# Half-block products of a hybrid attention layer: block sums taken out from beside them, one of four sums added by VectorE

## The chip, the cores and the metric

The kernel runs on one core of a Trainium2 chip. The metric is the device time of one execution in microseconds. Five engines work side by side, each in its own order: TensorE (PE, the matmuls, and PEld, its weight loads), VectorE (DVE), ScalarE (ACT), GpSimd (POOL) and SyncE (SP). SP issues nearly all DMAs, POOL those that accumulate in flight or write operands away to DRAM. Each engine waits in front of an instruction until its operands and buffers are there, and everything behind it waits too.

## What is computed

One decoder layer on 512 tokens of width 2048, in float32: RMS norm, one input projection, eight heads of latent attention (MLA) and eight of forgetting attention (FoX), each gated with SiLU, one output projection, RMS norm, residual.

```python
h = rms_norm(x, g_pre)
q_lat, kv_lat, k_rope, gate_mla, fq, fk, fv, f_logit, gate_fox = split(h @ w_in)
q  = rms_norm(q_lat, g_q) @ w_uq
kv = rms_norm(kv_lat, g_kv) @ w_ukv
o_mla = causal_attention(q, rope(k_rope), kv) * silu(gate_mla)
o_fox = forgetting_attention(fq, fk, fv, f_logit) * silu(gate_fox)
out = x + rms_norm(concat(o_mla, o_fox) @ w_out, g_post)
```

## The kernel before

Every float32 matmul is three matmuls of rounded parts: an operand is split into a high part (ACT casts it, `whi` for weights) and the rest (DVE subtracts, `wlo`), and `mm3` (lines 138 to 140) multiplies high by high, high by low and low by high. Weights arrive in chunks of 128 x 1024, 512 KB each: SP loads chunk i into one of three `raw` buffers (`load`), `divide` makes `whi` and `wlo` of it, of which there are three buffers each as well. A chunk feeds PE for some 2.8 us in the products and is loaded up to five chunks ahead in program order; a buffer comes free when the subtraction of the chunk three before it is done.

The work goes in five stages: the FoX heads in four pairs (up to 406 us in the profile), the last two latent blocks (to 434), the products for the other latents ("l") and the MLA gates ("m") (to 598), MLA in four head pairs (from 598 to 748), and the output projection (from 738 on, overlapping).

The products for l, m and for the two halves of the output ("0" and "1") are done with seven half-block products instead of eight. With weight blocks b11, b12, b21, b22 and operand blocks a11 to a22 (halves of the tokens and of the inner dimension) the weights' sums are

- t7 = b12 + b22, t5 = b11 + b12, t6 = b11 + t7, t4 = b21 + t6,

and the products p1 and p2 use plain blocks, p4 uses t4, q6 uses t6, g5 uses t5, g7 uses t7 and g3 a plain block. A product has four chunks, j = 0 to 3, and eight k-steps.

The weights' sums are made in DRAM, in the background. `sum_blocks` puts one entry (to, first, second) per sum and chunk on the list `bg`, 64 in all, in the order t7, t5, t6, t4 for each j, first l, then m, then the output. `add_step(n)` does three things: POOL issues the accumulate of entry n-1 (line 287, second added in flight to what was copied), SP issues the copy of entry n (line 290), and SP writes 16 elements of a weight tile that has just been used over the start of entry n+1 (line 292, the mark). The copy of the next step must wait for that mark to land, and the mark for that tile's cast, so the steps keep pace with the matmuls. `paced` calls `add_step` once every `pace` k-steps: 6 in the FoX stage, 4 at the last latents, 1000 (never) for most of the products of l and m, 6 again from m's g5 on, 3 from the end of m's g3 to the end. That makes 41 steps before the products of l and m, 4 in m's last three products, 13 in MLA and 8 in the first output products.

Operands take a similar way. Where the attention outputs are ready early, `away_steps` writes them and their differences to DRAM (POOL, line 871). `fetch` loads one back on SP (line 895, tiles `b...`, for the output `boa`: a11, a12, a22, for the latents' sums `bmq` and `bmg`), and `part_fetched` splits it in place on ACT and DVE (lines 129 and 130). These steps are queued in `todo`, and `pump` takes one or two of them at each k-step; a scheduler then fixes the order of each engine from the program's order and its own estimates, so that an instruction may move some places up or down.

The MLA gates (`gm`, lines 1236 to 1238: PE transposes into `gmt`, ACT takes the tanh, DVE multiplies) are queued at the end of m's products and run while pair 0's q projection (`mq`) runs. In MLA, a pair's scores (`sm`, line 591), exponentials (`pm`, line 608, ACT), transposes (`ptm`) and values (`pvm`) run beside the projections of the next pair. There are three PSUM banks for scores, so a pair's fourth score block waits until the exponential of the first has been taken.

Of the kernel before, what the change touches and what calls it, by code (L numbers as in the profile page):

```python
# [63 lines left out]
def tile_hybrid_layer(  # L64
# [16 lines left out]
    nc = tc.nc  # L81
# [133 lines left out]
    def load(i, small=None):  # L215

        w, cols, k, n, width = chunks[i]
        if cols is None:

            raw = raw_tile(i)  # L220
            nc.sync.dma_start(raw, w)
            raws[i] = raw
            return
        if i < 2:
            raw = slot(f"raw{i}", shape=(P, 1024))
        else:
            raw = raw_tile(i)
        v = raw[:, : n * width].rearrange("p (k c) -> p k c", k=n)
        for at, off, cnt in cols:
            (nc.sync if cnt >= P or small is None else small).dma_start(  # L230
                v[:, :, at : at + cnt],
                w[0, k * P : (k + n) * P, off : off + cnt].rearrange("(k p) c -> p k c", p=P),
            )
        raws[i] = raw

    def divide(i):
        w, cols, k, n, width = chunks[i]
        m = n * width
        raw = raws.pop(i)
        hi = wp.tile([P, 1024], F32R, tag="whi", name=f"whi{i}")  # L240
        lo = wp.tile([P, 1024], F32R, tag="wlo", name=f"wlo{i}")
        act.copy(hi[:, :m], raw[:, :m])  # L242
        dve.tensor_tensor(out=lo[:, :m], in0=raw[:, :m], in1=hi[:, :m].bitcast(F32), op=ALU.subtract)  # L243
        ready[i] = [t[:, :m].rearrange("p (k c) -> p k c", k=n) for t in (hi, lo)]
# [46 lines left out]
        if n + 1 < len(bg):  # L291
            nc.sync.dma_start(bg[n + 1][0][0:1, 0:16], mark)

    def sum_blocks(g, block):

        for name in ("t7", "t6", "t4", "t5"):

# [1 line left out]
        for j in range(4):  # L299
            b11, b12, b21, b22 = (block(j, h, c) for h in range(2) for c in range(2))  # L300
            t7, t6 = (W[n, g][j].rearrange("p (k c) -> p k c", k=2) for n in ("t7", "t6"))
            for name, first, second in (("t7", b12, b22), ("t5", b11, b12), ("t6", b11, t7), ("t4", b21, t6)):
                bg.append((W[name, g][j], first, second))

    prods = {}

    def add_products(names, plain):
# [3 lines left out]
        for name, g in names:  # L311
            first = len(chunks)
            if name in blocks:
                plain(g, *blocks[name])
            else:
                chunks.extend((W[sums[name], g][j], None, 0, 2, 512) for j in range(4))
            prods[name, g] = range(first, len(chunks))

    AT = {"l": 0, "m": O_GM}
# [4 lines left out]
        return w_in[0, k * P : (k + 2) * P, off : off + 512].rearrange("(k p) c -> p k c", p=P)  # L324

    for g in "lm":
        sum_blocks(g, lambda j, h, c, g=g: in_block(g, j, h, c))
    add_products(
        [
            *((n, g) for n in ("p1", "p2", "p4") for g in "lm"),  # L330
# [960 lines left out]
    product("q6", "m", operand("q6", "m"), C, True, True)  # L1291
    c12 = slot("gc12")
    scaled(c12, C, 0, pa, ALU.subtract)
    set_pace(6)
    product("g5", "m", operand("g5", "m"), G, True, True)
    c22 = slot("gc22")
    scaled(c22, G, 2, pb, ALU.subtract)
# [7 lines left out]
    todo.append(lambda: scaled(c12, G, 0, c12))  # L1305
    for f in range(4, 8):
        todo.append(lambda f=f: gate(f, c12, c22))
    set_pace(3)
    for n in ("a11", "a12"):
        for f in fetches(n, "o"):  # L1310
            f()
    qnh, qnl = zip(*(latents[i] for i in range(6)))
    knh, knl = zip(*(latents[i] for i in range(6, 10)))

# [1 line left out]
    for p in range(4):  # L1316
        c = mla[p]
        if p == 1:
            todo.extendleft([*divisions("a11", "o"), *divisions("a12", "o")])
        qb = [proj_bank(f"mq{p}{i}") for i in range(3)]  # L1320

# [5 lines left out]
        for i in range(2):  # L1327
# [5 lines left out]
                )  # L1333
            q[i].append(split(r, f"rq{p}{i}", first=P))
            qw[i].append(whole_block(wholes, 4 + i, r))
        kb = [proj_bank(f"mk{p}{i}") for i in range(2)]
        vb = [proj_bank(f"mv{p}{i}") for i in range(2)]

# [134 lines left out]
            square(t0 + t, c, o[t])  # L1473
            gain(t0 + t, c, o[t], homes.get(t0 + t))

    set_pace(3)
    gps = [slot(f"gp{c}") for c in range(2)]

    def load_gp(c):
# [21 lines left out]
            s()  # L1501

    product("p2", 0, operand("a12", "o"), A, False, True, 2, (6, heads_end))
    assert state["step"] > len(bg) and not later
    inner.close()
    op = ctx.enter_context(tc.tile_pool(name="op", bufs=8, reuse_waits="tile"))
    more.extend([op, state["loaded"]])
# [88 lines left out]
```

## Time and profile before

| | before |
|---|---|
| median of 3 runs | 926.26 us (924.95 to 929.02) |
| profiled execution | 925.18 us |
| its span, first to last instruction | 923.4 us |
| granted TensorE clock, mean | 0.993 |
| PE busy | 902.2 us, 98% |
| DVE busy | 619.2 us, 67% |
| ACT busy | 424.2 us, 46% |
| DMA moved | 203.6 MB, mean 220 GB/s |

Times of single instructions are given as the start from the span's begin and the length; square brackets at the end of a row say how long the engine was idle before it and which instruction ended that. `x4` means that four like instructions follow one another. In the list of waits the three numbers are the sum, the count and the longest. In the table by stretches of time the columns are the stretch and its length, then for each engine the busy time and the count, the granted clock, the share of the DMA engines' time and the rate. A matmul's length includes the pipeline, so consecutive ones overlap; how far their starts lie apart (0.23 us for 512 columns at full clock) is what each costs.

### The profile page before, as it was taken

The page shows a single profiled execution, that of the slowest core. Times are in us where ns is not written, and L with a number is a line of the kernel's source. Part 1 is how long each engine was busy: PE and PEld are TensorE (multiplying, and loading weights), DVE is VectorE, ACT ScalarE, POOL GpSimd, SP SyncE. Part 2 cuts the span into 40 slices and gives each one's busy share as a digit, 9 for nine tenths or more (in the row PEclk, how much of TensorE's full clock was granted, in tenths as well). Part 3 has the DMA queues.
Part 4 walks back from the last instruction along what each step waited for, and adds up shares of the span by engine and source line. Part 5 has one row for each costly group of instructions (what it writes and reads, how often), then busy time and mean ns, then how long its engine had stood idle before and what let it go on. Part 6 is the DMA issues. An engine that isn't in the chain of part 4 may idle for free.

```text
span 923.4 us, 12965 instructions
## 1 busy us (share of the span) xinstructions
PE 902.2 (98%) x4732; PEld 775.7 (84%) x4732; DVE 619.2 (67%) x1066; ACT 424.2 (46%) x779; POOL 87.2 (9%) x105
## 2 busy tenths in 40 slices
PE   9999999999999999999999999889999989999997
PEld 8988888998889888888999998768888868678885
DVE  4476878457462855554756777967887975696676
ACT  6762433243221442333564555644544545455474
POOL 1010111111111011111000000101101001000021
PEclk9999999999999999999999999989999999999999
DMA  9387897987998898897877767989857569887868
GB/s 300 91 206 209 230 221 194 250 208 191 226 273 198 222 253 205 208 242 183 294 245 239 235 182 209 259 224 219 194 125 186 150 186 271 278 260 232 274 192 250
DMA packets 122532, 203.60 MB, mean 220 GB/s; under 512 B 16194, under 2 KB 59740, under 8 KB 122468
## 3 DMA queue, kind: packets, MB, share of 16 engines
q1 hardware_dynamic: 105060, 158.85, 54.4%
q0 software_dynamic: 16672, 43.52, 25.7%
q8 instruction: 37, 0.61, 0.3%
q10 hardware_dynamic: 736, 0.40, 0.2%
q14 instruction: 27, 0.22, 0.1%
HBM read 190.66 MB, written 79.19 MB: 292 GB/s over the span
## 4 chain that ended last, share of the span: by engine, by line
PE 86%; DMA 7%; DVE 4%; ACT 2%; issue 1%; SPq 0%; ACTq 0%; DVEq 0%
PE fv L548 4%; PE fg L138 3%; PE fq L140 3%; PE fq L138 3%; PE fq L139 3%; PE fg L140 3%; PE fg L139 3%; PE fk L140 3%; PE fk L139 3%; PE fk L138 3%; DMA raw<-t 2%; PE fv L140 2%; PE fv L139 2%; PE fv L138 2%; DMA boa<-awayoa 2%; PE sm L591 2%
## 5 line engine op out<-in xcount | busy, mean ns | idle before, releaser
L243 DVE TENSOR_TENSOR wlo<-raw,whi 128x1024 fp32r<-128x1024 f32 (+3 forms) x205 | 243.0, 1187 | 186.3 <-ACT whi L242 178.5
L242 ACT CAST whi<-raw 128x1024 fp32r<-128x1024 f32 (+3 forms) x205 | 209.4, 1022 | 296.7 <-PE fk L139 52.9
L138 PE MATMUL fq<-h,whi 128*128 128x512 f32 x128 | 52.6, 411 | 0.0
L138 PE MATMUL fg<-h,whi 128*128 128x512 f32 x128 | 50.9, 398 | 0.0
L140 PE MATMUL fq<-h,wlo 128*128 128x512 f32 x128 | 50.3, 393 | 0.0
L139 PE MATMUL fq<-h,whi 128*128 128x512 f32 x128 | 50.1, 391 | 0.0
L140 PE MATMUL fg<-h,wlo 128*128 128x512 f32 x128 | 50.1, 391 | 0.0
L138 PE MATMUL fk<-h,whi 128*128 128x512 f32 x128 | 50.0, 391 | 0.0
L139 PE MATMUL fg<-h,whi 128*128 128x512 f32 x128 | 49.9, 390 | 0.0
L139 PE MATMUL fk<-h,whi 128*128 128x512 f32 x128 | 49.8, 389 | 0.0
L140 PE MATMUL fk<-h,wlo 128*128 128x512 f32 x128 | 49.8, 389 | 0.0
L287 POOL DMA_DIRECT2D t<-in_w_out_dram x16 | 18.4, 1152 | 240.6 <-DMA t<-in_w_out_dram 219.2
L140 PE MATMUL fv<-whi,h 128*128 128x256 f32 (+1 forms) x128 | 39.5, 309 | 0.0
L139 PE MATMUL fv<-wlo,h 128*128 128x256 f32 (+1 forms) x128 | 39.5, 309 | 0.0
L138 PE MATMUL fv<-whi,h 128*128 128x256 f32 (+1 forms) x128 | 39.5, 309 | 0.0
L548 PE MATMUL fv<-whi,h 128*128 128x456 f32 x128 | 37.6, 378 | 0.0
L138 PE MATMUL mq<-ln,whi 128*128 128x512 f32 x72 | 29.7, 415 | 1.6 <-ACT gm L1237 1.6
L608 ACT ACTIVATE pm<-sm,stm 128x128 f32<-128x128 f32 (+3 forms) x32 | 16.9, 528 | 27.6 <-DVE stm L606 27.6
L608 ACT ACTIVATE pf<-sf,stf 128x128 f32<-128x128 f32 (+3 forms) x32 | 16.9, 528 | 26.9 <-DVE stf L606 26.9
L140 PE MATMUL mq<-ln,wlo 128*128 128x512 f32 x72 | 29.2, 408 | 0.0
L139 PE MATMUL mq<-ln,whi 128*128 128x512 f32 x72 | 29.1, 404 | 0.0
L140 PEld LDWEIGHTS fq<-h,wlo 128*128 128x128 f32 x128 | 24.0, 188 | 5.4
(526 smaller groups left out, 2462.3 us busy)
## 6 DMA issues: line engine op xcount, KB each, us to landing
raw<-in_w_in_dram SPq DMA_DIRECT2D x80, 512.0 KB
t<-in_w_out_dram SPq DMA_DIRECT2D x32, 512.0 KB
raw<-t SPq DMA_DIRECT2D x32, 512.0 KB
raw<-in_w_out_dram SPq DMA_DIRECT2D x24, 512.0 KB
t<-in_w_out_dram POOLq DMA_DIRECT2D x16, 512.0 KB, 8.1
t<-t POOLq DMA_DIRECT2D x16, 512.0 KB, 6.6
awaymg<-rmg POOLq DMA_DIRECT2D x8, 512.0 KB, 8.3
raw<-in_w_ukv_dram SPq DMA_DIRECT2D x8, 512.0 KB
```

Of the source, the lines that this page charges most:

```text
L138: pe.matmul(o, ah, bh, start=first, stop=False, **kw)
L139: pe.matmul(o, ah, bl, start=False, stop=False, **kw)
L140: pe.matmul(o, al, bh, start=False, stop=last, **kw)
L242: act.copy(hi[:, :m], raw[:, :m])
L243: dve.tensor_tensor(out=lo[:, :m], in0=raw[:, :m], in1=hi[:, :m].bitcast(F32), op=ALU.subtract)
L287: pool.dma_start(to.rearrange("p (k c) -> p k c", k=2), second, accum_op=ALU.add)
L548: pe.matmul(banks[t][:, :n], a[k][:, tss[t]], b[:, j, :], start=k == 0 and m == 0, stop=k == NK - 1 and m == 2,)
L591: pe.matmul(s[:, :nn], a[:, qs], c[:, :nn], start=(i == 0), stop=(i == len(pairs) - 1))
L608: act.activation(p, s[:, :n], AF.Exp, bias=st[:, 0:1], accum_out=st[:, 1:2])
```

## The change

Four things change.

- t4 of l and m is no longer made in DRAM. `sum_blocks(..., late=True)` leaves it off `bg` (56 entries are left) and notes the pair (t6, b21) instead. `load` brings both to the chip, t6 into the `raw` buffer and b21 into a new tile `second` of the shared pool of 28 slots, and `divide` adds them on DVE in place before the cast.
- No steps beside m's g5, g7 and g3: `set_pace(6)` there is gone, the pace stays 1000.
- The steps that are left run in MLA alone: pace 2 from the end of pair 0's q projection on, 17 steps in the 34 k-steps that follow, and none beside the output products. Before the products of l and m there are 41 steps as before; since 8 entries of l and m are gone, those 41 reach 8 entries further into the output's sums.
- The four fetches of a11 and a12 are issued at the start of pair 1 instead of before MLA, and their divisions are queued at the start of pair 2 instead of pair 1.

```diff
@@ load
             raws[i] = raw
+            if k is not None:
+                second = slot(f"second{i}")
+                nc.sync.dma_start(second, k)
+                raws[i] = raw, second.rearrange("p k c -> p (k c)")
             return
@@ divide
         raw = raws.pop(i)
+        if isinstance(raw, tuple):
+            raw, second = raw
+            dve.tensor_tensor(out=raw, in0=raw, in1=second, op=ALU.add)
         hi = wp.tile([P, 1024], F32R, tag="whi", name=f"whi{i}")
@@ sum_blocks
-    def sum_blocks(g, block):
+    def sum_blocks(g, block, late=False):
...
-                bg.append((W[name, g][j], first, second))
+                if name == "t4" and late:
+                    W[name, g][j] = (W["t6", g][j], b21)
+                else:
+                    bg.append((W[name, g][j], first, second))
@@ add_products
-                chunks.extend((W[sums[name], g][j], None, 0, 2, 512) for j in range(4))
+                for j in range(4):
+                    w = W[sums[name], g][j]
+                    w, second = w if isinstance(w, tuple) else (w, None)
+                    chunks.append((w, None, second, 2, 512))
@@ for g in "lm"
-        sum_blocks(g, lambda j, h, c, g=g: in_block(g, j, h, c))
+        sum_blocks(g, lambda j, h, c, g=g: in_block(g, j, h, c), late=True)
@@ before m's g5
-    set_pace(6)
@@ after m's g3
-    set_pace(3)
-    for n in ("a11", "a12"):
-        for f in fetches(n, "o"):
-            f()
@@ for p in range(4), MLA
         if p == 1:
+            for f in (*fetches("a11", "o"), *fetches("a12", "o")):
+                f()
+        if p == 2:
             todo.extendleft([*divisions("a11", "o"), *divisions("a12", "o")])
@@ after pair p's q projection
+        if p == 0:
+            set_pace(2)
@@ before the output products
-    set_pace(3)
+    assert state["step"] > len(bg) and not later
@@ after p2 of output half 0
-    assert state["step"] > len(bg) and not later
```

How this moves instructions shows at three places. First DVE at p4 of l and the start of p4 of m (chunks 89 to 92 and 93 to 96; 87 and 88 belong to p2 of m before it). Before:

```order
L243 TENSOR_TENSOR wlo87_4351<-raw87_4280,whi87_4350 128x1024
L243 TENSOR_TENSOR wlo88_4369<-raw88_4312,whi88_4368 128x1024
L243 TENSOR_TENSOR wlo89_4387<-raw89_4348,whi89_4386 128x1024
L243 TENSOR_TENSOR wlo90_4405<-raw90_4366,whi90_4404 128x1024
L243 TENSOR_TENSOR wlo91_4430<-raw91_4384,whi91_4429 128x1024
L130 TENSOR_TENSOR bmg50_4575<-bmg50_4575 128x512
L243 TENSOR_TENSOR wlo92_4462<-raw92_4402,whi92_4461 128x1024
```

And now, on the same engine:

```order
L250 TENSOR_TENSOR wlo87_4353<-raw87_4280,whi87_4352 128x1024
L250 TENSOR_TENSOR wlo88_4373<-raw88_4312,whi88_4372 128x1024
L246 TENSOR_TENSOR raw89_4348<-raw89_4348,second89_4350 128x1024
L250 TENSOR_TENSOR wlo89_4394<-raw89_4348,whi89_4393 128x1024
L246 TENSOR_TENSOR raw90_4368<-raw90_4368,second90_4370 128x1024
L246 TENSOR_TENSOR raw91_4388<-raw91_4388,second91_4390 128x1024
L250 TENSOR_TENSOR wlo90_4415<-raw90_4368,whi90_4414 128x1024
L250 TENSOR_TENSOR wlo91_4443<-raw91_4388,whi91_4442 128x1024
L246 TENSOR_TENSOR raw92_4409<-raw92_4409,second92_4411 128x1024
L250 TENSOR_TENSOR wlo92_4478<-raw92_4409,whi92_4477 128x1024
```

Each chunk has an add in front, and the add of chunk 91 stands ahead of the subtraction of chunk 90; the split of the fetched operand `bmg50` has moved behind p4 of m.

Second, ACT at the divisions of the fetched a11 and a12 (`boa110` to `boa121`). Before, they stand in the middle of the gates at the entry of MLA:

```order
L1237 ACTIVATE gm1_5646<-gmt3_5654 128x512
L129 CAST boa110_5661<-boa110_5661 128x512
L129 CAST boa111_5663<-boa111_5663 128x512
L129 CAST boa120_5665<-boa120_5665 128x512
L129 CAST boa121_5667<-boa121_5667 128x512
L1237 ACTIVATE gm2_5689<-gmt4_5690 128x512
L242 CAST whi132_5726<-raw132_5608 128x1024
```

Now, on the same engine, they stand among the first exponentials of pair 0's heads, while pair 1's q projection runs:

```order
L129 CAST boa110_5935<-boa110_5935 128x512
L1031 COPY mv03_5927<-mv01_5819 128x256
L129 CAST boa111_5937<-boa111_5937 128x512
L621 ACTIVATE pm00_5967,stm00_5965<-sm00_5961,stm00_5965 128x128
L129 CAST boa120_5939<-boa120_5939 128x512
L621 ACTIVATE pm01_5980,stm01_5978<-sm01_5971,stm01_5978 128x256
L129 CAST boa121_5941<-boa121_5941 128x512
L249 CAST whi137_6027<-raw137_5868 128x1024
L621 ACTIVATE pm02_6002,stm02_6000<-sm02_5993,stm02_6000 128x384
L621 ACTIVATE pm03_6015,stm03_6013<-sm03_6006,stm03_6013 128x512
```

So the gates have no fetched operand between them any more, and the exponentials `pm00` to `pm02` have (`pm02` is score block 2 of head 0, `whi137` the first chunk of pair 1's w_ukv).

Third, SP in the first output products, where the sums of output half 0 (`t40..`) and half 1 (`t41..`) are loaded into `raw`. Before:

```order
L290 DMA t613_160<-in_w_out_dram 128x2x512
L230 DMA raw160_7509<-in_w_out_dram 128x2x512
L292 DMA t413_164<-whi157_7482 1x16
L221 DMA raw161_7539<-t400_145 128x1024
L290 DMA t413_164<-in_w_out_dram 128x2x512
L221 DMA raw165_7643<-t410_161 128x1024
L221 DMA raw162_7562<-t401_146 128x1024
```

And now:

```order
L234 DMA raw160_7518<-in_w_out_dram 128x2x512
L221 DMA raw161_7545<-t400_145 128x1024
L221 DMA raw165_7643<-t410_161 128x1024
L221 DMA raw162_7565<-t401_146 128x1024
L221 DMA raw166_7673<-t411_162 128x1024
```

The last copies and marks of the block sums (up to `t413`, the last entry of the list) no longer stand between the weight loads.

## Prediction

> **What bounds the kernel now.** I read the page first: busy times, clock, DMA share.
>
> ```profile
> PE 902.2 (98%) x4732; PEld 775.7 (84%) x4732; DVE 619.2 (67%) x1066; ACT 424.2 (46%) x779; POOL 87.2 (9%) x105
> ...
> DMA  9387897987998898897877767989857569887868
> GB/s 300 91 206 209 230 221 194 250 208 191 226 273 198 222 253 205 208 242 183 294 245 239 235 182 209 259 224 219 194 125 186 150 186 271 278 260 232 274 192 250
> ...
> q1 hardware_dynamic: 105060, 158.85, 54.4%
> q0 software_dynamic: 16672, 43.52, 25.7%
> ```
>
> TensorE (PE) is busy 98% of 923.4 us and the change neither adds nor removes a matmul. So only the other 2% can be won: PE's waits, and what the clock loses after a wait. The waits, in total and longest first:
>
> ```profile
> PE sm L591 <- ACT pm L608: 3.8, 1, 3.8
> PE gmt L1236 <- DVE gm L1238: 3.1, 1, 3.1
> PE ob L139 <- DVE wlo L243: 2.0, 3, 0.8
> PE mix L1437 <- ACT scaler L1436: 1.9, 1, 1.9
> PE mq L138 <- ACT gm L1237: 1.6, 1, 1.6
> ...
> PE gmt L1236 <- DVE gc L1220: 1.0, 1, 1.0
> PE ob L138 <- ACT whi L242: 0.4, 1, 0.4
> ```
>
> All but `mix` (at the end, untouched) lie between 575 and 815 us, where the change moves block sums and fetches. By stage (PE, PEld, DVE, ACT, POOL busy, then clock, DMA share, GB/s):
>
> ```profile
> 475.00:500.00 25.00, 25.00 (x157) 22.68 (x156) 14.75 (x16) 13.10 (x15) 0.00 (x0) 1.00 0.72 230
> 600.00:625.00 25.00, 21.87 (x105) 17.98 (x105) 17.34 (x26) 9.60 (x17) 1.98 (x2) 0.86 0.85 216
> 625.00:750.00 125.00, 123.20 (x704) 106.86 (x702) 102.28 (x217) 62.86 (x157) 11.84 (x12) 1.00 0.74 180
> 750.00:775.00 25.00, 22.64 (x108) 18.89 (x109) 17.45 (x36) 14.82 (x30) 2.08 (x3) 0.93 0.74 208
> 775.00:800.00 25.00, 24.20 (x107) 19.02 (x105) 12.07 (x14) 11.18 (x17) 2.67 (x3) 1.00 0.97 293
> 800.00:825.00 25.00, 23.38 (x97) 17.86 (x98) 24.03 (x32) 15.77 (x22) 0.00 (x0) 1.00 0.79 254
> ```
>
> Three places lose time; the p4 stage (479 to 501 us) now loses none.
>
> **A. Entry of MLA: the a11 and a12 fetches, moved by one head pair.** SP issues four fetches; ACT and DVE, which work in order, come to their division before the data, and the gates behind them are late for PE:
>
> ```profile
> 598.30 1.85 SPq L895 DMA_DIRECT2D boa<-awayoa  x4
> ...
> 603.75 1.27 ACT L129 CAST boa<-boa 128x512 fp32r<-128x512 f32 x2 [2.22 <-DMA boa<-awayoa]
> ...
> 608.39 0.62 ACT L129 CAST boa<-boa 128x512 fp32r<-128x512 f32 x1 [1.05 <-DMA boa<-awayoa]
> ...
> 610.39 1.12 PE L1236 MATMUL gmt<-ident,gc 128*128 128x128 f32 x4 [3.13 <-DVE gm L1238]
> ...
> 611.15 0.78 PE L140 MATMUL mq<-ln,wlo 128*128 128x512 f32 x1
> ...
> 612.15 0.63 PE L139 MATMUL mq<-ln,whi 128*128 128x512 f32 x1
> ...
> 616.27 0.39 PE L140 MATMUL mq<-ln,wlo 128*128 128x512 f32 x1
> ```
>
> PE stands 3.1 us, and the clock is then halved: the 12 matmuls from 611.15 to 616.27 start 0.43 us apart instead of 0.23, 2.4 us more. With the divisions gone from there, nothing else at this place waits for the fetch: gain 5.5 us. The other two waits at the entry, 1.0 and 1.6 us, come from a full DVE queue that the four removed block-sum steps lighten only by way of earlier loads; I take half, 1.3 (ends 0 and 2.6).
>
> Where the four fetches go: in the new order SP issues them behind the pair-1 loads of w_ukv (in before from 627.59 to 629.33), and their casts stand on ACT ahead of the softmax exponentials of head 0.
>
> ```profile
> 627.59 1.74 SPq L230 DMA_DIRECT2D raw<-in_w_ukv_dram  x2
> ...
> 630.74 0.40 PE L138 MATMUL mq<-ln,whi 128*128 128x512 f32 x1
> ```
>
> At A the last cast began 10.1 us after the first issue (598.30 to 608.39), the first pair's 5.5 us after. From 629.3 that is 639.4 and 634.8. The exponential of score block 2 of head 0 stands behind the fourth boa cast (0.62) and one `whi` cast (1.05): not before 641.1. PE, which has 27 `mq` matmuls (0.23 each, 6.2 us) and six score blocks (some 3 us) between 630.74 and the score block that needs that bank, comes there at about 640. A wait of about 2 us, with ends 0 (the fetches land sooner) and 5.5 (the same as at A, clock included). I take 2.0, nearer to what the two times give than to either end. Behind these casts stand the `whi` cast and the subtraction of pair 1's w_ukv, which PE needs only after the whole q projection.
>
> **B. The a22 fetch after MLA**, same code, but its rivals for the DMA engines go.
>
> ```profile
> 741.70 1.02 SPq L895 DMA_DIRECT2D boa<-awayoa  x2
> ...
> 751.11 0.62 ACT L129 CAST boa<-boa 128x512 fp32r<-128x512 f32 x1 [5.00 <-DMA boa<-awayoa]
> ...
> 752.36 0.82 PE L591 MATMUL sm<-mk,mq 128*128 128x256 f32 x3 [3.76 <-ACT pm L608]
> ```
>
> The fetch took 9.4 us beside a block copy and an accumulate; ACT stood 5.0 us with the exponentials behind it, PE 3.8 us. Clock 0.93 in 750 to 775 is 3.5 us at half rate, 1.7 us lost. Without block sums there the fetch should take what the first one at A took, 5.5 us, and ACT's 5.0 us wait shrinks to 1.1: PE does not stand. Gain 5.5 (ends 0, where the exponentials are late anyhow, and 5.5). What is late next there is DVE (row maxima and `boa`), by tenths.
>
> **C. First output products.** The last accumulate starts only when PE is in `ob`, and SP stands in front of the load that needs it, with all later loads behind:
>
> ```profile
> 780.46 18.75 SPq L221 DMA_DIRECT2D raw<-t  x8
> ...
> 790.11 0.81 POOL L287 DMA_DIRECT2D t<-t  x1 [8.52 <-PE oa L139]
> ...
> 791.84 1.05 ACT L242 CAST whi<-raw 128x1024 fp32r<-128x1024 f32 x1 [5.18 <-DMA raw<-t]
> ```
>
> DMA is at its limit there (0.97). After the change the last block sum ends in MLA, so the eight `raw<-t` loads follow one another at once. They remain 4.2 MB, so the stage stays dense. PE's waits here are 2.0 + 0.4; with the matmuls being restarted up to 4.8 us. I take 2.4 (ends 0 and 4.8).
>
> **D. What is added: p4 of latents and gates from two loads and a sum.** Eight times 0.52 MB more, and eight adds on DVE; an add of 128x1024 costs what the subtraction of that size does.
>
> ```profile
> 467.96 5.74 SPq L221 DMA_DIRECT2D raw<-t4l  x3
> ...
> 479.00 0.28 PE L138 MATMUL gbl<-h,whi 128*128 128x256 f32 x1
> ...
> 480.86 1.23 DVE L243 TENSOR_TENSOR wlo<-raw,whi 128x1024 fp32r<-128x1024 f32 x1 [2.06 <-ACT whi L242]
> ...
> 481.95 1.05 ACT L242 CAST whi<-raw 128x1024 fp32r<-128x1024 f32 x1 [0.61 <-PE gbl L139]
> ...
> 490.51 0.40 PE L138 MATMUL gbm<-whi,h 128*128 128x512 f32 x1
> ...
> 501.42 0.28 PE L138 MATMUL gcl<-bmq,whi 128*128 128x256 f32 x1
> ```
>
> DVE has 14.75 of 25 us busy in 475 to 500; 8 x 1.23 = 9.8 us more leaves it just below full, so DVE itself is not the bound, but each add waits for a DMA, and in the new order adds of later chunks stand ahead of the subtractions of earlier ones. Time budget: PE starts p4 at 479.00, the m half at 490.51, the next product at 501.42; a chunk of m takes 2.73 us, so the last starts at 498.69. Ahead of it stand add 1.23, cast 1.05, subtraction 1.23: its data must be there at 495.2, that is 27.2 us after the first p4 load at 467.96. Eight pairs are 8.39 MB: at 308 GB/s they fit exactly. The best slice of the page shows 300 GB/s. With the two chunk loads still in flight at 467.96 it is 9.44 MB, at 300 GB/s 31.5 us: 4.3 us late. Lower end 0, if nothing was in flight. For the upper end, a load from the dense stage at C, from the chain of waits (start, length):
>
> ```profile
> 777.76 7.74 DMA raw<-t
> ```
>
> Three `raw` buffers make a loop of load, add, cast and subtraction; with such a load it is 11.2 us per three chunks, 3.7 each against 2.8, 7.6 over eight chunks, and 9 with the operand fetches for g5 that now follow behind. I take 3.0, nearer to the 4.3 of the page's rate than to 0, and spread over several chunks: like the `ob` waits (0.8 at most, clock 1.00 in their windows) each is too short to halve the clock. The eight second loads need tiles of the shared pool of 28; SP stands if the last reader of such a tile isn't done, with the raw loads behind it. The eight h tiles that only p1 reads are free by then, so I cost that at nothing; if it isn't so, it is part of rival 2.
>
> By the Trainium skill, "DMA: Bandwidth & Descriptors", Specifications, one core's HBM limit is about 358 GB/s. By that D would cost nothing, 9.44 MB taking 26.4 us, and the sum would be 3 us lower; no slice here shows more than 300, so I stay with the row.
>
> **E. Block sums moved into MLA.** From the page's queues: hardware queue 0.544 x 923.4 / 158.85 = 3.16 us of all 16 engines per MB, software queue 0.257 x 923.4 / 43.52 = 5.45. A step (copy and accumulate, 0.52 MB each) is 1.66 + 2.86 = 4.5 us. Eight steps fall away, 36 us of DMA, eight loads come, 13 us. In 625 to 750 the share is 0.74; pace 2 instead of 3 makes 5 steps per head pair of 10 k-steps instead of 3.3 in 37 us ((741.70 - 630.74) / 3): 1.67 x 4.5 / 37 = 0.20 more, 0.94. A chunk of weights there is used every 7 us with three ahead, so slower loads stay covered: cost 1.0 (ends 0 and 5). SP's marks and copies wait about 2 us for each other with the weight loads behind them, which the same three chunks cover; POOL's accumulates run later than the copies, but nothing in MLA reads them. In m's g5, g7 and g3 four steps go, which PE never waited for directly.
> The earlier place of every sum of w_out in the attention stages costs nothing: the number of steps there stays 41, and no wait of the list falls there.
>
> **Sum.** Gains 5.5 + 1.3 + 5.5 + 2.4 = 14.7; costs 3.0 + 2.0 + 1.0 = 6.0; net -8.7. The profiled execution took 925.18 us for its span of 923.4; the median of the three runs is 926.26, 1.1 above it. 925.2 - 8.7 + 1.1 = 917.6, forecast 917.5.
>
> **Rivals.**
> 1. D and the moved fetch are hidden: two loads in flight have landed by 467.96, the boa fetch is as fast as at B without block sums. All ends at gain: 926.3 - 14.7 + 1 = 912.5, at best 926.3 - 18.4 = 908. For it: 11 us of lead from 467.96 to 479.00; against: 300 GB/s. The Trainium skill's rule named at D speaks for this case too.
> 2. The gain is eaten: p4 loses 9, the moved boa fetch 5.5 (its ACT stall merely changes place, since the same four fetches stand in front of the same kind of chain). 926.3 - 14.7 + 14.5 + 1 = 927; with one of the two at half, 922.5. This is also the case in which the change does not do what it says, freeing the product stages of DMA only to load the p4 stage.
> 3. Slower: in MLA the DMA engines are full. The computed share is 0.94; beside block sums the fetch of B took 9.4 us, and at 0.97 a load 7.7. If SP's raw loads come late once in each 25 us of 625 to 750, with a wait like A's of 3.1 us, that is 5 x 3.1 = 15.7 us: 917.6 - 1 + 15.7 = 932. It passes 926.3 from 1.9 us per 25 us on, and 930.9 from 2.9. For it: 0.94 and in-order SP; against: now 1.8 us of PE idle in all 125 us at 0.74, and three chunks ahead.
>
> **Chances.** Forecast 0.48, rival 1 0.20, rival 2 0.17, rival 3 0.15. A measurement here tells some 0.5% from no change, 4.6 us: below 921.6 is faster. Forecast and rival 1 are there but for a little, rival 2 lies within 0.5% but for 0.03 that are slower, rival 3 above it but for 0.01: faster 0.68, same 0.15, slower 0.17. The range takes rival 1's best and reaches towards rival 3: 908 to 929. The forecast's own, with the ends of D and the moved fetch: 912 to 922.
>
> **What would show it.** A right: no wait of `gmt` on `gm` near 605, clock 1.00 there. B: no `sm` wait on `pm` at a22, the fetch about 5 us. C: no `ob` waits, no accumulate after 760. D right: `gbl` or `gbm` matmuls wait on `wlo` for a few us in all, DMA share about 0.95 from 470 to 495. Moved fetch: one wait of `sm` on `pm` in pair 1. E: MLA share about 0.9 without waits on `whi`. I am wrong if `gbm` waits exceed 6 us, or if `mq` and `mk` wait for `whi` or `wlo` throughout MLA.

## The result

| | before | after |
|---|---|---|
| median | 926.37 us (924.86 to 929.02, 6 runs) | 917.27 us (914.46 to 919.42, 6 runs) |
| ratio to before, 95% interval | | 0.9896 (0.9872 to 0.9921) |
| profiled execution / its span | 925.18 / 923.4 us | 916.44 / 914.5 us |
| granted TensorE clock, mean | 0.993 | 0.996 |
| DMA moved | 203.6 MB | 199.4 MB |

The changed kernel is 1.0% faster, 9 us, and forecast (917.5) and time agree to 0.3 us. The terms behind it agree less well, as the experiments show.

From the page of the changed kernel: PE works 3.6 us less for the same 4732 matmuls (its busy time counts the slow clock too), DVE 7 us more; the software queue lost 4.2 MB.

```profile
PE 898.6 (98%) x4732; PEld 774.3 (85%) x4732; DVE 626.4 (69%) x1074; ACT 423.6 (46%) x779; POOL 80.5 (9%) x97
...
DMA  9378888997997898989789965549999436787878
GB/s 302 93 201 214 232 215 193 239 228 193 225 273 183 199 253 208 235 209 223 249 303 302 305 195 171 163 125 260 206 231 223 119 118 199 239 257 221 271 193 251
...
q1 hardware_dynamic: 105044, 158.84, 55.4%
q0 software_dynamic: 15520, 39.33, 23.4%
```

Its list of PE's waits (sum, count, longest). `gmt` on `gm` and all `ob` waits are gone. The wait of `sm` on `pm` is another one than before: not at a22 but at 636 us, in pair 1. Two `gbm` waits are new.

```profile
PE sm L604 <- ACT pm L621: 2.6, 1, 2.6
...
PE mq L138 <- DVE gc L1233: 1.6, 1, 1.6
PE gbm L139 <- DVE wlo L250: 1.3, 2, 0.8
...
PE pvf L139 <- DVE plf L130: 0.9, 1, 0.9
```

By stretches (columns as before). PE is full from 745 to 795 us, where before it lost time from 750 on. It stays full to 825. The p4 stage is at 306 GB/s and MLA's share is 0.82.

```profile
475.00:500.00 25.00, 23.68 (x147) 20.66 (x146) 18.70 (x17) 9.34 (x10) 0.00 (x0) 1.00 0.89 306
620.00:745.00 125.00, 122.02 (x694) 105.96 (x694) 101.87 (x214) 64.25 (x159) 13.52 (x14) 0.99 0.82 200
745.00:770.00 25.00, 25.00 (x126) 20.23 (x126) 20.10 (x45) 15.16 (x34) 0.00 (x0) 1.00 0.50 158
770.00:795.00 25.00, 25.00 (x115) 20.74 (x115) 17.68 (x22) 15.12 (x23) 0.00 (x0) 1.00 0.70 235
```

To see waits and slow clock in one number, I add up over each trace how much later every matmul starts than the one before it allows at full clock (0.23 us for 512 columns, 0.12 for 256, and so on). This "lost PE time" is 36.9 us before and 28.0 after; the difference, 8.9, is that of the spans. By place (A1 is the 5.5 us of the prediction's A for the wait on the fetch, A2 its 1.3 for the other two waits there):

| place | lost before | lost after | difference | the prediction's term |
|---|---|---|---|---|
| MLA's entry, 575 to 625 us | 10.1 | 2.6 | -7.5 | A1 + A2: -6.8 |
| pair 1, 625 to 650 | 0.5 | 5.1 | +4.6 | moved fetch: +2.0 |
| rest of MLA, 650 to 725 | 2.7 | 2.9 | +0.2 | E: +1.0 |
| a22, 725 to 775 | 6.8 | 1.8 | -5.0 | B: -5.5 |
| first output products, 775 to 825 | 4.8 | -0.1 | -4.9 | C: -2.4 |
| p4, 475 to 500 | 0.1 | 2.3 | +2.2 | D: +3.0 |
| FoX, 325 to 350 | 0.4 | 1.6 | +1.2 | none |

The last row is the wait of `pvf` on `plf`. Of the runs below whose code is the same there, two lose 1.4 and 1.6 us at that place and the others 0.3 to 0.5: it changes from execution to execution and is no effect of the change.

The new wait in pair 1, from the timelines of SP, ACT and PE: SP issues the four fetches from 625.71 on, the first cast starts 8.6 us later, and ACT stands 5.5 us with head 0's exponentials behind it. PE then stands 2.59 us, and the seven `mq` matmuls from 637.66 to 640.22 us each start 0.43 us after the one before.

```profile
625.71 2.97 SPq L908 DMA_DIRECT2D boa<-awayoa  x4
...
634.28 0.62 ACT L129 CAST boa<-boa 128x512 fp32r<-128x512 f32 x1 [5.53 <-DMA boa<-awayoa]
...
635.59 0.37 ACT L621 ACTIVATE pm<-sm,stm 128x128 f32<-128x128 f32 x1
...
636.10 0.96 PE L604 MATMUL sm<-mk,mq 128*128 128x512 f32 x3 [2.59 <-ACT pm L621]
...
639.80 0.63 PE L140 MATMUL mq<-ln,wlo 128*128 128x512 f32 x1
```

### The profile page after: what moved, and what is told of

The parts are those of the page before. It is cut to its first block, busy times and chain, and to the rows that moved or that the text cites. A ratio compares the mean times of both kernels' runs of the same rounds, so it can differ in the third digit from the quotient of the medians.

```text
span 914.5 us, 12937 instructions
## 1 busy us (share of the span) xinstructions
PE 898.6 (98%) x4732; PEld 774.3 (85%) x4732; DVE 626.4 (69%) x1074; ACT 423.6 (46%) x779; POOL 80.5 (9%) x97
## 4 chain that ended last, share of the span: by engine, by line
PE 55%; DVE 4%; DMA 2%; ACT 1%; issue 0%; SPq 0%; DVEq 0%; ACTq 0%
PE sm L604 2%; PE mq L138 2%; PE mq L140 2%; PE mq L139 2%; PE oa L140 2%; PE oa L138 2%; PE oa L139 2%; PE od L139 2%; PE oc L139 2%; PE od L138 2%; PE oc L140 2%; PE oc L138 2%; PE od L140 2%; DVE wlo L250 1%; DMA boa<-awayoa 1%; PE ptm L630 1%
## 5 line engine op out<-in xcount | busy, mean ns | idle before, releaser
L140 PEld LDWEIGHTS fg<-h,wlo 128*128 128x128 f32 x128 | 24.0, 188 | 5.3
```

The source lines that it names most:

```text
L140: pe.matmul(o, al, bh, start=False, stop=last, **kw)
```

## The experiments

Ratios are to the kernel before, run on the same chip in the same series; the changed kernel has 0.9896, from its own series.

### One part alone and one part undone: the moved fetch

The kernel before with only the fetch moved (`moved_alone`), and the changed kernel with it put back (`fetch_back`):

```diff
@@ moved_alone, from the kernel before
     set_pace(3)
-    for n in ("a11", "a12"):
-        for f in fetches(n, "o"):
-            f()
...
         if p == 1:
+            for f in (*fetches("a11", "o"), *fetches("a12", "o")):
+                f()
+        if p == 2:
             todo.extendleft([*divisions("a11", "o"), *divisions("a12", "o")])
@@ fetch_back, from the changed kernel: the same lines the other way round
```

> The kernel before with only the four fetches of a11 and a12 and their divisions moved by one head pair; the block sums, their paces and t4 stay as before. Theory: at MLA's entry the wait of gmt on gm (3.1 us) and the half clock behind it (2.4) go, with them part of the two other waits there (1.0 and 1.6), together 5.5 to 8; in pair 1 the wait of sm on pm comes with its slow clock, as in the changed kernel, about 4.6. Net 1 to 3 us faster than before, 923.5 to 925.5. Rival, the wait only changes place: 926, with a pair-1 wait longer than 3 us since block sums share the DMA engines there. Rival, most of the whole gain of 9 us is A's: below 920.

> The changed kernel with the fetches put back ahead of MLA and the divisions back to pair 1; everything else as changed, so no block sums run at MLA's entry. Theory: the wait of gmt on gm comes back whole and the pair-1 wait goes: 917.3 + 7.5 - 4.6 = 920. Rival, what made A's fetch slow were the block sums beside it, not its place: without them it takes about 5 us as at B, gmt waits 1 us or less, and the time is 917.3 - 4.6 + 1 = 914, faster than the changed kernel.

Measured: `moved_alone` 1.0053 (1.0031 to 1.0076), 930.61 us, slower than before; `fetch_back` 0.9855 (0.9828 to 0.9882), 913.66 us, faster than the changed kernel. The theory falls in both: `moved_alone` has the long pair-1 wait of its first rival and a time beyond it, and `fetch_back` shows its rival.

Waits of `moved_alone`: the entry's 3.1 us are gone, but `sm` waits twice, 4.7 us in pair 1 (and 4.1 at a22 as ever).

```profile
PE sm L591 <- ACT pm L608: 8.8, 2, 4.7
```

In ACT's timeline the fetch, issued at 623.11 beside block sums at pace 3, lets the first cast begin after 9.1 us and the third after 12.7.

```profile
632.18 0.62 ACT L129 CAST boa<-boa 128x512 fp32r<-128x512 f32 x1 [6.05 <-DMA boa<-awayoa]
...
635.82 0.62 ACT L129 CAST boa<-boa 128x512 fp32r<-128x512 f32 x1 [0.31 <-DMA boa<-awayoa]
```

In `fetch_back` the fetch stands where it stood before, but no block sums run there. In its waits 0.6 of `gmt`'s 3.1 us are left:

```profile
PE gmt L1249 <- DVE gm L1251: 0.6, 1, 0.6
```

In its timelines of SP and ACT the four casts run in one row, 5.2 us after the issue:

```profile
598.24 1.88 SPq L908 DMA_DIRECT2D boa<-awayoa  x4
...
603.43 2.69 ACT L129 CAST boa<-boa 128x512 fp32r<-128x512 f32 x4 [2.25 <-DMA boa<-awayoa]
```

So A was lost to the block sums beside the fetch, not to its place (`late_sum_alone` below, which differs from `fetch_back` by the paces alone, keeps the wait). Taking them away was enough; moving the fetch as well costs 0.4% (0.9896 against 0.9855, 3.8 us), and 0.5% where the sums stay. The two intervals of the 0.4% still overlap by 0.001, but the traces say the same: 5.1 us lost from 625 to 650 in the changed kernel, 0.9 in `fetch_back`.

### What makes the fetch slow in pair 1, and what it holds up

`sums_later` starts the block sums only after pair 1's q projection, then at pace 1.4; `late_casts` leaves the fetch and holds only its casts, behind the last exponential of head 1 in ACT's order (`exps` lists the instructions of the exponentials as they are written).

```diff
@@ sums_later, from the changed kernel
-        if p == 0:
-            set_pace(2)
+        if p == 1:
+            set_pace(1.4)
@@ late_casts, from the changed kernel
+            def after_exps(f):
+                with tc.issue_after(exps[-1]):
+                    f()
+
-            todo.extendleft([*divisions("a11", "o"), *divisions("a12", "o")])
+            todo.extendleft([lambda f=f: after_exps(f) for n in ("a11", "a12") for f in divisions(n, "o")])
```

> The changed kernel with no block sums before pair 1's k and v projection, and then all 17 steps at pace 1.4. The fetch of a11 and a12 in pair 1 so has only the weights' loads beside it. Theory: block sums make that fetch slow: the first cast begins 5 to 6 us after the first issue instead of 8.6, the wait of sm on pm near 636 is under 1 us. Rival: the loads of the weights do it, fetch and wait stay at about 8.5 and 2.5 us. What follows at pace 1.4 tells on E: at pace 1 it cost some 20 us, at pace 2 nothing; lost PE time between 645 and 720 above 5 us puts the limit between 1.4 and 2, below 2 us under 1.4.

> The changed kernel with the fetches where they are, and only the ACT casts of a11 and a12 held behind the last exponential of head 1 in ACT's order. Theory: the pair-1 loss is ACT standing at the casts with the exponentials behind; then the wait of sm on pm at 636 (2.6 us) and the slow clock behind it (about 2) go: 917.3 - 4.6 = 912.7. Rival: the exponentials are late for another reason (row maxima on DVE, the whi cast): the wait stays at 1.5 us or more, 915 to 917.

`sums_later`: 0.9916 (0.9884 to 0.9948). SP issues the fetch at 627.23, and the first cast comes 5.6 us later instead of 8.6; ACT stands 2.6 us instead of 5.5, PE 0.84 instead of 2.59, and lost PE time from 625 to 650 is 1.7 us instead of 5.1. The block sums, not the weights, make it slow, as at the entry. Timelines of SP, ACT and PE, the last row from pair 3:

```profile
627.23 1.85 SPq L908 DMA_DIRECT2D boa<-awayoa  x4
...
632.78 0.62 ACT L129 CAST boa<-boa 128x512 fp32r<-128x512 f32 x1 [2.56 <-DMA boa<-awayoa]
...
639.47 0.62 PE L604 MATMUL sm<-mk,mq 128*128 128x256 f32 x3 [0.84 <-ACT pm L621]
...
714.01 0.63 PE L604 MATMUL sm<-mk,mq 128*128 128x256 f32 x3 [1.58 <-ACT pm L621]
```

Its time can't be told from the changed kernel's. In the trace, the 3.4 us won in pair 1 are given back: from 700 to 725 us, where the sums now run at pace 1.4, it loses 2.7 us against 0.9, and the start of the program and p4, which the edit doesn't touch, lose 1.1 and 0.4 more in this execution.

`late_casts`: 0.9836 (0.9808 to 0.9864), 910.89 us, 0.6% below the changed kernel, as the theory said. The fetch is as slow as ever; nothing waits for it. No `sm` wait is in its list, and the stretch is full, with the DMA engines at 0.99:

```profile
620.00:645.00 25.00, 25.00 (x133) 21.42 (x132) 20.00 (x51) 15.08 (x39) 3.10 (x3) 1.00 0.99 262
```

### The sum from two loads alone, and the paces

`late_sum_alone` is the kernel before with the late t4 and nothing else; `pace3` is the changed kernel with pace 3 in MLA and the output.

```diff
@@ late_sum_alone: load, divide, sum_blocks(late=True) and add_products as in the change;
@@ set_pace(6), set_pace(3) and the fetches as before
@@ pace3, from the changed kernel
-            set_pace(2)
+            set_pace(3)
...
-    assert state["step"] > len(bg) and not later
+    set_pace(3)
```

> The kernel before with t4 of l and m from two loads and an add, and nothing else: paces and fetches as before, so 4 block-sum steps stay beside m's g5, g7 and g3, the rest runs at pace 3 from MLA's entry and ends in MLA. Theory: B and C gain as in the changed kernel (about 5 each), D costs its 3 us, and A stays, since block sums still run beside the fetch at the entry: about 918 to 920, that is 5 to 8 us above the run with the fetches put back. Rival: the paces do nothing, the entry loses its wait here too because the sums are thinner: 912 to 914.5. Rival: B stays, since the sums end too late: above 922.

> The changed kernel with pace 3 instead of 2 in MLA and on into the output: 11 of the 17 steps run in MLA, 6 beside the a22 fetch and the first output products. Theory: of the kernel before's losses B (wait of sm on pm at a22, 4 to 5 us with its slow clock) and most of C (ob waits, 3 to 5) come back, 915.6 + 7 to 10 = 922 to 926. Rival: B's and C's loss came from the whole of the block sums, earlier ones too, and 6 steps bring back little: 917 to 919.

`late_sum_alone`: 0.9909 (0.9884 to 0.9933), 918.89 us, as expected. The block sums end at 711 us, so B and C are won (lost PE time 1.6 us from 725 to 775, -0.1 after), while A stays whole, since its sums still run at the entry: 10.5 us lost from 575 to 625, a new wait of 1.8 us in m's last product (`gdm`) among them. Its waits:

```profile
PE gmt L1249 <- DVE gm L1251: 3.3, 1, 3.3
...
PE gdm L139 <- DVE wlo L250: 1.8, 1, 1.8
PE gbm L139 <- DVE wlo L250: 1.8, 1, 1.8
```

So the eight sums fewer carry nearly the whole net gain of the change. Leaving the entry free of block sums (`fetch_back` differs from this run by the paces alone) gives another 0.5%, and the moved fetch takes 0.4% of it away again.

`pace3`: 0.9941 (0.9917 to 0.9966), 0.45% slower than the changed kernel, 4 us, about half of what I expected. The profiled execution, 925.11 us, is near the slowest of the eight and loses 3 us more than the changed kernel's at the start of the program, which the edit doesn't touch. By stretches B is back and C is not: the last accumulate is issued at 778.82 us, and although the DMA engines are then at 0.99 and 315 GB/s, PE is full.

```profile
745.00:770.00 25.00, 21.28 (x107) 17.89 (x106) 16.91 (x45) 12.42 (x30) 3.14 (x3) 0.93 0.74 186
770.00:795.00 25.00, 25.00 (x120) 20.73 (x119) 15.63 (x19) 14.26 (x22) 0.81 (x1) 1.00 0.99 315
```

So a dense DMA alone does not cost C. Before, the last accumulate was issued 11 us later (790.11), and the `raw<-t` loads stood behind it.

### How dense the block sums may be

`pace1` is `late_casts` with pace 1 in MLA.

```diff
-            set_pace(2)
+            set_pace(1)
```

> The changed kernel with the held casts and pace 1 instead of 2 in MLA: the 17 block-sum steps run in 17 k-steps, so at twice the density. It looks for the point from which E costs. Theory: three chunks ahead cover it and the wait of a step for its mark keeps SP from more than the DMA engines take: whi waits of 2 us in all at most, 910 to 912. Rival 3 of the prediction as a mechanism (full DMA engines, late weights): a wait of about 3 us in each of two or three stretches of 25 us, 916 to 920.

Measured 1.0051 (1.0028 to 1.0074), 931.59 us: 2%, some 20 us, above `late_casts`, where rival 3 of the prediction gave 15.7. Stretches, then SP, ACT and PE at the first place, and the next two late casts on ACT:

```profile
620.00:645.00 25.00, 20.71 (x110) 18.05 (x111) 15.97 (x39) 10.22 (x27) 4.83 (x5) 0.91 1.04 247
645.00:670.00 25.00, 22.11 (x117) 19.11 (x117) 16.64 (x30) 10.82 (x25) 3.97 (x4) 0.89 0.95 222
670.00:695.00 25.00, 19.03 (x91) 15.54 (x90) 12.45 (x27) 7.50 (x18) 4.00 (x4) 0.86 1.05 255
```

```profile
624.24 0.40 SPq L234 DMA_DIRECT2D raw<-in_w_ukv_dram  x1
...
631.09 0.38 SPq L234 DMA_DIRECT2D raw<-in_w_ukv_dram  x1
...
637.92 1.04 ACT L249 CAST whi<-raw 128x1024 fp32r<-128x1024 f32 x1 [6.10 <-PE sm L606]
641.12 0.58 ACT L623 ACTIVATE pm<-sm,stm 128x384 f32<-128x384 f32 x1 [2.15 <-DVE stm L621]
...
641.84 1.01 PE L606 MATMUL sm<-mk,mq 128*128 128x256 f32 x3 [4.25 <-ACT pm L623]
...
650.62 1.05 ACT L249 CAST whi<-raw 128x1024 fp32r<-128x1024 f32 x1 [5.88 <-DMA t<-whi]
...
688.02 1.04 ACT L249 CAST whi<-raw 128x1024 fp32r<-128x1024 f32 x1 [11.01 <-DMA raw<-in_w_ukv_dram]
```

The two loads of `w_ukv` for pair 1, which follow one another in `late_casts` (620.04, x2), are 6.9 us apart here: between them stand the fetch and, in the stream ahead, block copies with their marks. The cast (`whi`) of such a chunk stands in ACT's order ahead of an exponential. ACT stood 6.1 us in front of it (the row names `sm`, which was long done, so it was something else), and PE waits 4.25 us for the exponential: not for weights, but for what the late weights hold up. The second late cast waits 5.88 us for a mark, the small copy out of a `whi` tile, and the third 11.01 us for its raw load. So of the three late casts in 75 us one is by its row the late raw load of rival 3, one is held by a step's mark, and the first stays open. In `late_casts`, at pace 2, the shares of these stretches are as high (0.99, 1.05, 0.99) with at most 0.4 us of PE idle, so a full share of the DMA engines alone doesn't tell when the loss begins.

### What the p4 stage pays for

`one_load` leaves out second loads and adds (t6 stands where t4 belongs, so the sums b21 are missing from the result), `loads_no_adds` keeps the loads alone (the same is missing), `adds_no_loads` has the adds alone, each t6 chunk added to itself (b21 is missing there too).

```diff
@@ one_load
-                second = slot(f"second{i}")
-                nc.sync.dma_start(second, k)
-                raws[i] = raw, second.rearrange("p k c -> p (k c)")
@@ loads_no_adds
-            dve.tensor_tensor(out=raw, in0=raw, in1=second, op=ALU.add)
@@ adds_no_loads
-                raws[i] = raw, second.rearrange("p k c -> p (k c)")
+                raws[i] = raw, raw
```

> The changed kernel without the second loads and without the adds: p4 of l and m uses t6 where t4 belongs, so that part of the computation is left out. It gives the whole price of D. Theory: the gbm waits of 1.3 us and the stretched matmuls around them go, 917.3 - 2.3 = 915.0, and the DMA rate from 470 to 497 falls below 250 GB/s. Rival 1 of the prediction (D hidden): 917, no difference. Rival, D also delays the operand fetches for g5 behind it: 913 or less.

> The changed kernel with the second loads of p4 but without the adds (t6 is used for t4, so that part of the computation is left out). D by DMA alone. Theory: what p4 loses is the transfers' time at about 303 GB/s: PE loses 1 to 2.5 us between 475 and 500 as with the adds, and the time is 914.5 to 916. Rival, D is the add on DVE and the longer chain load, add, cast, subtraction on three raw buffers: the loss falls under 0.3 us and the time to that without the loads, 913.

> The changed kernel with the adds but without the second loads: each t6 chunk is added to itself, so t4 is wrong and that part of the computation is left out. D by DVE alone. Theory: 9.8 us more on DVE are hidden, PE loses under 0.3 us between 475 and 500, 913. Rival, the chain on three raw buffers: 1 to 2.5 us lost there, 914.5 to 916.

Measured: 0.9863 (0.9837 to 0.9888), 0.9868 (0.9845 to 0.9891) and 0.9886 (0.9860 to 0.9911). The whole price is 0.9896 - 0.9863, 3 us with an interval that reaches from about nothing to 6; in lost PE time from 475 to 500 us it is 2.3 against 0.1. The parts cost next to nothing each: 0.1 us lost with the loads alone, and 0.1 with the adds alone, with 0.4 more just behind 500. The stretch in the two runs, loads alone first:

```profile
475.00:500.00 25.00, 25.00 (x157) 22.64 (x157) 12.86 (x12) 11.09 (x13) 0.00 (x0) 1.00 0.99 360
```

```profile
475.00:500.00 25.00, 25.00 (x157) 22.61 (x156) 21.82 (x22) 11.80 (x14) 0.00 (x0) 1.00 0.64 211
```

The DMA engines move 360 GB/s here when they are asked to, so the 306 of the changed kernel are not their limit, and the theory that the transfers' time alone is what p4 pays falls. But nothing in `loads_no_adds` waits for a second load, so it doesn't show that a late one costs nothing once there is an add. What the changed kernel's timelines of SP, DVE, ACT and PE show is a chain, and in it a wait for a second load:

```profile
483.97 1.22 DVE L246 TENSOR_TENSOR raw<-raw,second 128x1024 f32<-128x1024 f32 x1
...
484.52 0.39 SPq L225 DMA_DIRECT2D second<-in_w_in_dram  x1
...
485.30 1.05 ACT L249 CAST whi<-raw 128x1024 fp32r<-128x1024 f32 x1 [2.50 <-DVE raw L246]
...
486.38 1.23 DVE L250 TENSOR_TENSOR wlo<-raw,whi 128x1024 fp32r<-128x1024 f32 x1 [1.19 <-ACT whi L249]
487.53 1.22 DVE L246 TENSOR_TENSOR raw<-raw,second 128x1024 f32<-128x1024 f32 x1
...
492.61 1.23 DVE L246 TENSOR_TENSOR raw<-raw,second 128x1024 f32<-128x1024 f32 x1 [1.45 <-DMA second<-in_w_in_dram]
...
496.31 0.51 PE L139 MATMUL gbm<-wlo,h 128*128 128x512 f32 x1 [0.76 <-DVE wlo L250]
```

Add, cast, subtraction, and then the next chunk's add, where it stands behind that subtraction in DVE's order: 3.56 us from add to add, where PE uses a chunk in 2.73. Not every add stands so; those of the third and the eighth chunk stand ahead of the subtraction of the chunk before. The chain uses up part of the lead, and the sixth chunk's second load then makes PE wait. It is issued at 484.52, when the third chunk's subtraction has freed a raw buffer, and the add stands 1.45 us for it; PE's wait of 0.76 us is for that chunk's subtraction. From the end of the third chunk's subtraction to that of the sixth's it is 12.2 us (484.06 to 496.26), where PE takes 8.2 for three chunks.

The other traces bear this out. In four of them PE waits once in p4, for the seventh chunk's subtraction, and ahead of that in DVE's order stands the eighth chunk's add, which waits for its second load: 0.22 us in `late_casts` (PE 0.38), 0.83 in `fetch_back` (0.99), 1.36 in `late_sum_alone` (1.82) and 2.31 in `pace3` (2.54). So p4 pays for the loop through the three raw buffers, of load, add, cast and subtraction, together with DVE's order. `loads_no_adds` and `adds_no_loads` each take one part out of the loop: in the first nothing waits for a second load, in the second there is none, and the scheduler put most adds ahead of the previous chunk's subtraction. How much of the price is the order alone is not shown by a run; the changed kernel with another order of the adds was not tried.

### Two attempts at a faster version

`both` is `late_casts` with each second load issued a chunk ahead, the first two before SP stands for a raw buffer. `half_late` adds to it that t4 of l comes from block sums again and that the 21 steps run at pace 1.9 from MLA's begin.

```diff
@@ both, from late_casts
-                second = slot(f"second{i}")
-                nc.sync.dma_start(second, k)
+                load_second(i)
+                load_second(i + 1)
@@ half_late, from both
-        sum_blocks(g, lambda j, h, c, g=g: in_block(g, j, h, c), late=True)
+        sum_blocks(g, lambda j, h, c, g=g: in_block(g, j, h, c), late=g == "m")
```

> The changed kernel with the casts of a11 and a12 held behind the exponentials, and the second loads of p4 issued one chunk ahead, the first two before SP stands for a raw buffer at 467. Theory: the data of each chunk is there before its add, the gbm waits (0.8 to 2.3 us lost between 475 and 500 in the runs so far) go: 910.0 - 1.5 = 908.5. Rival: the DMA engines at 303 GB/s are the limit of that stage, and earlier seconds only delay the other loads: 910, the same as with the held casts alone.

> The changed kernel with held casts and earlier second loads, the sum from two loads for m alone (t4 of l is made by block sums again), and pace 1.9 from MLA's begin so that 21 steps fit there. Theory: p4 has 2.1 MB less to load in 27 us, PE loses under 0.5 us between 475 and 500: 910 - 1.5 = 908.5. Rival: the four steps more at MLA's begin (before the fetch of pair 1, at a DMA share near 1) cost as much as p4 gives: 910 or more.

`both`: 0.9826 (0.9801 to 0.9851), not to be told from `late_casts`; p4 still loses 2.6 us (`late_casts` 0.8, `fetch_back` 1.4 in their executions), so earlier seconds do not help it: the adds wait for their raw loads instead, up to 2.67 us at 488.27. `half_late`: 0.9845 (0.9817 to 0.9873). p4 loses 0.1 us, as expected, and the rival takes it back: with the steps from MLA's begin a `whi` cast waits 4.15 us for its raw load in pair 1 (ACT's timeline), and the wait of `sm` on `pm` that holding the casts had removed is there again.

```profile
631.62 1.05 ACT L260 CAST whi<-raw 128x1024 fp32r<-128x1024 f32 x1 [4.15 <-DMA raw<-in_w_ukv_dram]
...
635.54 0.72 PE L619 MATMUL sm<-mk,mq 128*128 128x256 f32 x3 [2.33 <-ACT pm L636]
```

`late_casts` and `both`, 0.983 and 1.6 to 1.7% below the kernel before, beat both given kernels.

## Why the prediction was right

The time is right to 0.3 us because errors of opposite sign cancel, above all the moved fetch (2.6 us too low a cost) and C (2.5 too low a gain), and that is luck. The mechanisms named are there in the main; the sizes are not. By its steps:

- **A1, A2.** Size 6.8, measured 7.5. Of A2's two waits that of 1.0 went and that of 1.6 (`mq`) stayed. The reason for A1 was half right. That "nothing else at this place waits for the fetch" holds for the changed kernel, but the prediction credited the gain to the move. In `fetch_back` the fetch stays and 0.6 us of its wait is left, so the block sums taken from m's last products and from MLA's entry are the cause. The prediction saw that argument at B ("its rivals for the DMA engines go") and didn't apply it at A.
- **Moved fetch.** The term most off: 2.0 taken, 4.6 measured, within the end of 5.5. The mechanism is the one described, casts ahead of head 0's exponentials. Mis-sized was the fetch: its first cast began 8.6 us after the issue, not the 5.5 taken from A, so that already the first exponential was late for PE (5.6 in `sums_later`, without block sums beside it). And the 2.0 is the wait alone, without the slow clock behind it.
- **B.** 5.5 against 5.0, by the step named: the fetch's first cast 4.6 us after its issue (741.95 to 746.50), no `sm` wait. `pace3`, which brings block sums back beside it, brings 4.9 us back (lost PE time 5.8 in 750 to 775 against 0.9).
- **C.** 2.4 taken, 4.9 measured, the upper end: the first `raw<-t` loads no longer wait, and all lost time went, not half.
- **D.** 3.0 taken, 2.2 measured: the size came near, but the reason it was taken from failed. The prediction's "at 300 GB/s 31.5 us: 4.3 us late" takes the best slice for a limit; 360 GB/s are to be had, and the kernel before already shows 323 from 770 to 795 us. By the Trainium skill, "DMA: Bandwidth & Descriptors", Specifications, one core's HBM limit is about 358 GB/s; the 360 in `loads_no_adds` reach that figure, against the row I preferred, and whether more can be had no run shows. Yet the conclusion drawn from it, no cost, did not come true either. What the traces show is the prediction's other reason, which it used for the upper end alone: the loop on three raw buffers, put at 11.2 us per three chunks, takes 12.2 at the chunk for which PE waits. That DVE's order stands in this loop was missed. The size changes with the execution: the eight kernels with these loads and adds lose 0.8 to 4.1 us there.
- **E.** 1.0 taken, 0.2 measured. While the sums run, from 625 to 720 us, the share is 0.95, as computed; over the 125 us it is 0.82, because the last accumulate is issued at 715 us, and from 720 to 745 the share is 0.30. At this density the cost is still near nothing. Rival 3's loss is real, but it begins beyond the change's density: at pace 1 it is 2%, at 1.4 a first wait of 1.6 us appears. And the share alone doesn't tell it. Its reason, late raw loads, is shown for one of the three late casts there.
- **Rival 2** (the stall merely changes place) is right for the moved fetch seen alone: `moved_alone` is 0.5% slower.
- **The list of waits.** "All but `mix`" holds for the rows shown; the full list has two waits of 1.1 us at the start of the program (`xt`, `warm`) that the change doesn't touch.

## What to carry to other kernels

When a transfer is late, ask what shares the DMA engines with it before moving it: taking the rivals away was enough here, and the move put a stall in front of a worse queue. A wait of an in-order engine costs what stands behind it; holding four casts behind the exponentials, with not one transfer changed, was worth 0.6%. And a term can be right in size for the wrong reason: a busiest slice is what was asked for, not what the engines can do, so look also for a loop that runs from a load over several engines and through the buffer back to the next load.

## What the hardware showed

The length of a wait does not decide alone whether the clock is lost. After 1.56 us (`mq` at MLA's entry, nearly every execution), 1.58 (`sums_later`, 714) and 1.66 (`moved_alone`, `pvm` at 776) it stayed whole; after every `sm` and `gmt` wait from 2.2 to 5.4 us the matmuls behind it came at about half the rate, seven or more of them. In between, a wait of 2.54 us at `gbm` (`pace3`, 502.47) cost nothing more, while one of 1.82 at the same tile (`late_sum_alone`, 498.93) was followed by seven matmuls 0.43 us apart, from 500.29 on.

The granted clock that the traces record says why. From 20 us on and ahead of the last 30 us, it is halved for 3.41 or 6.83 us at a time, and in one run these stretches begin whole multiples of 3.41 us apart (`late_sum_alone`: 500.07, 599.06 and 616.12). Cut at these steps, the two waits differ (`late_sum_alone` first, then `pace3`; the clock is the third figure from the end):

```profile
496.66:500.07 3.41, 1.59 (x7) 0.97 (x7) 3.36 (x4) 2.22 (x3) 0.00 (x0) 1.00 0.99 309
500.07:503.48 3.41, 3.41 (x10) 2.64 (x9) 3.41 (x6) 2.16 (x5) 0.00 (x0) 0.50 0.89 262
```

```profile
498.00:501.41 3.41, 1.93 (x9) 1.26 (x7) 1.35 (x2) 0.92 (x2) 0.00 (x0) 1.00 0.95 333
501.41:504.83 3.42, 2.36 (x10) 1.95 (x11) 3.37 (x4) 3.42 (x5) 0.00 (x0) 1.00 0.73 239
```

The wait of 1.82 us lies in one step, that of 2.54 is divided into 1.48 and 1.06 us. Over all 14 traces, each of the 17 steps at full clock in which PE idles 1.82 us or more is followed by a step at half clock, and none in which it idles 1.71 us or less. So about half a step of idling decides, in these runs.

By the Trainium skill, "TensorE: Matmul & The Clock Gate", Part 1, a free-running window of about 3.4 us decides, and the half rate comes after at least one idle window. The traces agree with the free-running window, by the steps of 3.41 us; that the whole window must be idle does not hold here, since 1.82 us did it.

A stretch in which the DMA engines are listed at 1.05 of their time lost nothing (`late_casts`, 645 to 670).
